# State mixing on 64 rows per head with swapped heads, and TensorE's queue in written order

## The chip, the cores and the metric

The kernel runs on one core of a Trainium2 chip. The metric is device time in microseconds (us) of one execution. Before the change three runs took 2027.13, 2028.16 and 2031.48 us; their median is 2028.16. Engines are called as the profile calls them: PE is TensorE's matmuls and PEld its weight loads, DVE is VectorE, ACT ScalarE, POOL GpSimd, SP the queue from which most transfers are issued.

## What is computed

The reference is a small two-layer transformer trunk over 256 context tokens and 512 latent tokens with 1024 features. The change lies in layer 0, where the mixer has two halves: attention with 8 query heads and 2 key heads, and an RWKV-7 recurrence with 8 heads in two directions over the same tokens. The recurrence keeps a 64x64 state S per head and direction:

```
S_t = S_{t-1} (diag(w_t) - kk_t^T (a_t * kk_t)) + v_t^T k_t ;  y_t = S_t r_t
scan(zero state, context) -> s_ctx ;  scan(s_ctx, latent)      # for d in (forward, reversed)
o = post(y_forward + y_reversed)                               # group norm, bonus, gate
```

Attention for query tiles of the context sees the context alone; for latent tiles it sees all 768 tokens, with a softmax over them.

## The kernel before

The stage in question (lines 882 to 1194) runs state mixing and attention together on TensorE, between the projections of layer 0 and its output projection. It takes the 768 tokens in 24 chunks of 32, two chunks making a block of 64 tokens; both directions go at once, the reversed one from the other end. In memory the 8 heads are 4 tiles of 128 rows, with two heads (h = 0, 1) in the two halves of 64 rows.

`prepare` (L943) loads a block's operands on SP and makes its products. For each direction and each half m of the head tiles, z (L981) multiplies the operands kb by ar. So that one product serves two heads, kb is laid out as a block matrix of 128x128 (the tiles `kbd`, zeroed once, filled by two loads of 64 rows each, L957). Two DVE products (L987) mask z, one into `zk` and one into `z`; ACT copies the rest (L990). xv (L998) multiplies zk by the values v. POOL copies and scales ar into `ard`, laid out as a block matrix too, in four products of 64 rows a block (L972).

`step` (L1007) is the chain from state to state. x (L1022) applies ard to the state, DVE adds xv and gives xs (L1025), u (L1032) applies a triangular inverse in 32x32 tiles, DVE adds v and gives vu (L1037, once per direction), s (L1047) makes the update in 64x64 tiles, and DVE adds it to the decayed old state (L1055), which POOL made (L1013). `outputs` (L1058) makes y from the state and from vu (L1066, L1068) and adds it into `yacc`. `finish` (L1088) normalizes, transposes (yt, L1112), gates and stores a pair of token tiles.

`attend` (L1123) does attention for one query tile: per key head g and query head j the scores sc (L1143, two or four matmuls into one buffer of two PSUM banks), a maximum on DVE (L1145), Exp on ACT (L1150), a scaling; then `weighted` (L323) transposes the probabilities four at a time (pt, L332), copies them out on ACT or DVE alternately (L335, L337), and multiplies them by the values into two halves of po (L341).

What orders the work: the kernel is written as generators. `state_mixing` (L1158) advances attention by 40 yields first and then by a yield here and there between the steps; `step` and the first `prepare` have high priority. The scheduler of the framework then chooses each engine's order by priority and by its own simulated time, so a matmul of any kind can go between two of another. PSUM has two buffers for z, xv, y and yt together, one for x, u and s, one for po, two for pt and one (of two banks) for sc.

Of the kernel before, what the change touches and what calls it, by code (L numbers as in the profile page):

```python
# [38 lines left out]
HALVES = (slice(0, 64), slice(64, 128))  # L39

# [36 lines left out]
def constants():  # L77
# [21 lines left out]
    head, slot = p // 64, (p // 32) % 2  # L99
    own = (head[:, None] == np.arange(2)[None, :])[:, :, None]  # L100
    for dr in (0, 1):
        isk = slot == dr
        sgn = np.where(isk, 1.0, -1.0).astype(f)
        if dr == 0:
            inc, exc = t[None, :] >= s[:, None], t[None, :] > s[:, None]
        else:
            inc, exc = t[None, :] <= s[:, None], t[None, :] < s[:, None]
        c.add(f"rmask{dr}", (own * inc[:, None, :] * sgn[:, None, None]).astype(f))
        c.add(f"kmask{dr}", (own * (exc & isk[:, None])[:, None, :]).astype(f))
        c.add(f"sgn{dr}", sgn)  # L110
        c.add(f"umask{dr}", (~isk).astype(f)[:, None])
# [113 lines left out]
def tile_trunk(ctx: ExitStack, tc: tile.TileContext, t: dict, out, cc: Cols, pc: Cols):  # L225
# [656 lines left out]
    with ExitStack() as sb:  # L882
        psum_pool(sb, zy=(2, 1), ch=(1, 1), po=(1, 1), pt=(2, 1), sc=(1, 2))
# [9 lines left out]
        for g in (0, 1):  # L893
# [3 lines left out]
            split(kh[:, g], kl[:, g], kraw)  # L897
        early = ExitStack()
# [17 lines left out]
        ard = [br.tile([P, 4, 2, 2, 64], F32, name=f"ard{n}") for n in range(5)]  # L916
        zts = [br.tile([P, 4, 2, P], F32, name=f"z{n}") for n in range(4)]
        for n in range(3):
            zero(kbd[n].rearrange("p a c n -> p (a c n)"), n > 1)
            V.tensor_tensor(out=ari[n].rearrange("p a c n -> p (a c) n")[:, :, 64:128], in0=ident[:, 0:64].unsqueeze(1).to_broadcast([P, 8, 64]),  # L920
                            in1=ident[:, 64:128].unsqueeze(1).to_broadcast([P, 8, 64]), op=ALU.add)
        for n in range(5):
            zero(ard[n].rearrange("p a c s n -> p (a c s n)"), n > 1)
# [4 lines left out]
        A.activation(func=AF.Copy, out=dds[:, 0:7, 1, :], in_=DD[1][:, :, 6::-1].rearrange("p a n -> p n a"))  # L928
        A.activation(func=AF.Copy, out=dds[:, 7:23, 1, :], in_=DD[1][:, :, 23:7:-1].rearrange("p a n -> p n a"))
# [13 lines left out]
        def prepare(b):  # L943
# [5 lines left out]
            for d in (0, 1):  # L949
# [3 lines left out]
                kb, ar, bd = kbd[n % 3], ari[n % 3], ard[n % 5]  # L953
                nc.sync.dma_start(ar[:, :, :, 0:64], arD[d][i][:, :, c:c + P].rearrange("q a (c n) -> q a c n", c=2))
                for h in (0, 1):
                    r = HALVES[h]
                    nc.sync.dma_start(kb[r, :, :, 64 * h:64 * h + 64], kbD[d][i, r, :, c:c + P].rearrange("q a (c n) -> q a c n", c=2))  # L957
                    v = vD[64 * blk[d]:64 * blk[d] + 64, h].rearrange("(j q) a e -> q j (a e)", j=2)
                    for j in (0, 1):
                        s = 32 * (2 * h + d)  # L960
                        nc.sync.dma_start(vm[d][s:s + 32, j].rearrange("q a e -> q (a e)"), v[:, 1 - j if d else j, :])
                ld.append((kb, ar))
# [3 lines left out]
            def run():  # L966
                zks = {}
                for d in (0, 1):
                    kb, ar = ld[d]
                    for h in (0, 1):  # L970
                        r = HALVES[h]
                        G.tensor_tensor(out=ars[d][r, :, :, :, 32 * h:32 * h + 32].rearrange("p a c s t -> p (a c) s t"),  # L972
                                        in0=ar[r, :, :, 0:64].rearrange("p a c (s t) -> p (a c) s t", s=2),
                                        in1=dsel[r, b, d].rearrange("p a c -> p (a c)").unsqueeze(2).unsqueeze(3).to_broadcast([64, 8, 2, 32]),
                                        op=ALU.mult)
                    for m in (0, 1):

                        ps = psum("zy", "z")
                        for a in (0, 1):
                            for c in (0, 1):  # L980
                                T.matmul(ps[:, P * (2 * a + c):P * (2 * a + c) + P], lhsT=kb[:, 2 * m + a, c, :], rhs=ar[:, 2 * m + a, c, :],  # L981
                                         start=True, stop=True)
                        pv = ps.rearrange("p (n x) -> p n x", x=P)
                        z = zs[d][:, 2 * m:2 * m + 2].rearrange("p a c x -> p (a c) x")
                        zk = bq.tile([P, 4, 64], F32, tag="zk", name=u("zk"), bufs=4)
                        for dst, c0, nm in ((zk, 32, "kmask"), (z[:, :, 0:64], 0, "rmask")):
                            V.tensor_tensor(out=dst.rearrange("p n (h t) -> p n h t", h=2),  # L987
                                            in0=pv[:, :, c0:c0 + 32].unsqueeze(2).to_broadcast([P, 4, 2, 32]),
                                            in1=K(f"{nm}{d}").rearrange("p (h t) -> p h t", h=2).unsqueeze(1).to_broadcast([P, 4, 2, 32]), op=ALU.mult)
                        A.activation(out=z[:, :, 64:128], in_=pv[:, :, 64:128], func=AF.Copy, scale=K(f"sgn{d}"))  # L990
                        zks[d, m] = zk
                        yield
                for j in (0, 1):
                    px = psum("zy", "xv")
                    for a in range(4):
                        for d in (0, 1):
                            c = 1 - j if d else j
                            T.matmul(px[64 * d:64 * d + 64, 64 * a:64 * a + 64], lhsT=zks[d, a // 2][:, 2 * (a % 2) + c, :], rhs=vm[d][:, j, a, :],  # L998
# [159 lines left out]
        def state_mixing(fill):  # L1158
# [26 lines left out]
            for _ in done:  # L1185
                pass
# [613 lines left out]
```

## Time and profile before

| what | us |
|---|---|
| profiled execution | 2029.69 |
| span of its instructions | 2027.9 |
| median of three runs | 2028.16 |
| PE busy (94% of the span) | 1900.6 |
| DVE busy | 1217.1 |
| ACT busy | 842.6 |
| POOL busy | 360.6 |

The mean granted TensorE clock was 0.975 of full speed. Times inside the span are counted from its first instruction. A float32 matmul appears as two instructions in the trace. An instruction's duration runs from its start to its last result, and matmuls overlap one another in the array, so what a matmul costs is read from one start to the next, not from its duration. A form such as 128*64 128x64 gives the rows and columns of the array that the matmul uses, and then the partitions and the elements that move through it.

### The profile page before, as it was taken

The numbers are of one execution on the slowest core, as the hardware profiler recorded it, in microseconds if no ns is written. First come the engines' busy times: TensorE is split into PE (matmuls) and PEld (weight loads), VectorE is DVE, ScalarE is ACT, GpSimd is POOL, SyncE is SP. The second block draws the span as 40 slices with busy tenths as digits, with TensorE's granted clock in tenths as the row PEclk, the third lists the DMA queues.
The fourth block names the chain that finished last, engine by engine and source line by source line (L and its number), as shares of the span: only waits on it lengthen the run. The fifth ranks groups of instructions, "written<-read, shape, count | busy, mean of one in ns | idle before, by whom it ended". The sixth has DMA issues, their size and how long they took to land.

```text
span 2027.9 us, 34250 instructions
## 1 busy us (share of the span) xinstructions
PE 1900.6 (94%) x13992; PEld 1547.3 (76%) x13992; DVE 1217.1 (60%) x2070; ACT 842.6 (42%) x1419; POOL 360.6 (18%) x371
## 2 busy tenths in 40 slices
PE   6999868899999899999999999899899799999997
PEld 4776647776765898888888889778668487888886
DVE  5577969575677675555544443865677464344436
ACT  4344432455554443332233224554566444333335
POOL 0022276333222430000000002310153120000002
PEclk9999979899999999999999999999899799999998
DMA  9346554842323643344444432212101133323333
GB/s 333 120 146 193 195 174 143 166 98 59 90 59 110 230 124 93 115 125 135 125 126 131 128 94 73 87 45 73 42 1 43 42 95 97 100 86 102 94 99 109
DMA packets 147885, 228.19 MB, mean 113 GB/s; under 512 B 65024, under 2 KB 102288, under 8 KB 147600
## 3 DMA queue, kind: packets, MB, share of 16 engines
q1 hardware_dynamic: 140912, 213.54, 35.8%
q10 hardware_dynamic: 5456, 7.73, 1.1%
q0 software_dynamic: 1360, 4.73, 0.7%
q8 instruction: 110, 1.80, 0.4%
q14 instruction: 47, 0.39, 0.1%
HBM read 200.00 MB, written 25.96 MB: 111 GB/s over the span
## 4 chain that ended last, share of the span: by engine, by line
PE 69%; DVE 13%; DMA 7%; ACT 4%; issue 4%; POOL 3%; SPq 0%; DVEq 0%; POOLq 0%; ACTq 0%
PE m L367 37%; PE win L367 9%; PE po L341 4%; DMA wmod<-in_wmod_dram 4%; PE pt L332 3%; PE z L981 2%; DVE wlo L280 2%; PE wout L1714 2%; PE wout L1298 2%; PE sc L1143 2%; DMA wraw<-in_win_dram 1%; PE z L1556 1%; DVE junk L1315 1%; PE s L1047 1%; DVE it L778 1%
## 5 line engine op out<-in xcount | busy, mean ns | idle before, releaser
L279 ACT ACTIVATE whi<-wraw 128x1024 fp32r<-128x1024 f32 x214 | 226.4, 1059 | 691.1 <-PE m L367 555.7
L280 DVE TENSOR_TENSOR wlo<-wraw,whi 128x1024 fp32r<-128x1024 f32 x214 | 263.7, 1234 | 204.3 <-ACT whi L279 201.5
L367 PE MATMUL m<-hh,whi 128*128 128x512 f32 (+1 forms) x816 | 239.6, 345 | 3.9 <-ACT relu L1237 2.4
L367 PE MATMUL m<-hh,wlo 128*128 128x512 f32 (+1 forms) x816 | 242.1, 345 | 0.4 <-DVE wlo L280 0.4
L367 PE MATMUL m<-hl,whi 128*128 128x512 f32 (+1 forms) x816 | 241.9, 344 | 0.2 <-POOL hl L503 0.2
L367 PE MATMUL m<-dh,whi 128*128 128x256 f32 (+1 forms) x832 | 238.9, 342 | 2.7 <-DVE xl L1219 2.5
L367 PE MATMUL m<-dl,whi 128*128 128x256 f32 (+1 forms) x832 | 241.1, 341 | 0.0
L367 PE MATMUL m<-dh,wlo 128*128 128x256 f32 (+1 forms) x832 | 240.0, 342 | 0.1
L471 POOL TENSOR_TENSOR acc<-acc,nsq 128x256 f32<-128x256 f32 x42 | 43.6, 1047 | 870.9 <-ACT nsq L470 867.0
L367 PEld LDWEIGHTS m<-dh,whi 128*128 128x128 f32 x832 | 153.4, 188 | 24.9 <-DVE xl L1219 6.2
L367 PEld LDWEIGHTS m<-hh,whi 128*128 128x128 f32 x816 | 152.4, 189 | 23.6 <-ACT relu L1237 2.8
L367 PEld LDWEIGHTS m<-hh,wlo 128*128 128x128 f32 x816 | 153.7, 189 | 20.0 <-DVE wlo L280 0.9
L367 PEld LDWEIGHTS m<-hl,whi 128*128 128x128 f32 x816 | 153.8, 189 | 19.2 <-POOL hl L503 0.4
L367 PEld LDWEIGHTS m<-dl,whi 128*128 128x128 f32 x832 | 154.0, 188 | 18.9
L367 PEld LDWEIGHTS m<-dh,wlo 128*128 128x128 f32 x832 | 153.8, 188 | 18.8 <-DVE wlo L280 0.3
L367 PE MATMUL win<-hl,whi 128*128 128x512 f32 (+1 forms) x512 | 162.2, 350 | 4.7 <-POOL hl L503 3.5
L367 PE MATMUL win<-hh,whi 128*128 128x512 f32 (+1 forms) x512 | 158.0, 355 | 8.6 <-DVE kr L381 5.6
L367 PE MATMUL win<-hh,wlo 128*128 128x512 f32 (+1 forms) x512 | 160.3, 347 | 1.8 <-DVE wlo L280 1.8
L1315 DVE SCALAR_TENSOR_TENSOR junk<-wmod,crow 128x1024 f32<-128x1024 f32 x64 | 78.4, 1225 | 119.0 <-DMA wmod<-in_wmod_dram 118.4
L1219 DVE SCALAR_TENSOR_TENSOR xl<-m,modT,xl 128x512 f32<-128x512 f32 (+1 forms) x144 | 97.3, 686 | 72.2 <-PE m L367 72.2
L367 PEld LDWEIGHTS win<-hh,whi 128*128 128x128 f32 x512 | 95.4, 194 | 31.2 <-issue 12.3
L367 PEld LDWEIGHTS win<-hl,whi 128*128 128x128 f32 x512 | 98.9, 194 | 21.1 <-POOL hl L503 4.7
(416 smaller groups left out, 3624.3 us busy)
## 6 DMA issues: line engine op xcount, KB each, us to landing
wraw<-in_w_dram SPq DMA_DIRECT2D x136, 512.0 KB, 3.6
wmod<-in_wmod_dram SPq DMA_DIRECT2D x96, 512.0 KB, 4.1
wraw<-in_wout_dram SPq DMA_DIRECT2D x40, 512.0 KB, 3.7
wraw<-in_win_dram SPq DMA_DIRECT2D x35, 512.0 KB, 4.0
arD<-ar SPq DMA_DIRECT2D x8, 768.0 KB, 4.2
kbD<-kb SPq DMA_DIRECT2D x8, 768.0 KB, 3.7
ari<-arD SPq DMA_DIRECT2D x24, 256.0 KB, 4.3
kbd<-kbD SPq DMA_DIRECT2D x48, 128.0 KB, 4.0
```

The source lines that it names most:

```text
L279: A.activation(out=hi, in_=src, func=AF.Copy)
L280: (lo_eng or V).tensor_tensor(out=lo, in0=src, in1=hi.bitcast(F32), op=ALU.subtract)
L332: T.transpose(pt[:, P * j:P * j + P], prob[j][:, P * m:P * m + P], ident)
L341: T.matmul(po[HALVES[i], :], lhsT=vt[:, k_, r], rhs=w_, start=m_ < 2, stop=m_ + 2 >= n, tile_position=(0, 64 * i))
L367: T.matmul(part(ps, s), lhsT=a[:, c], rhs=row(b, k, s), start=first and j == 0 and q == 0, stop=last and j == n - 1 and q == 2)
L471: (V if k == KT - 1 else eng).tensor_tensor(out=at(acc, s), in0=at(acc, s), in1=at(sq, s), op=ALU.add)
L981: T.matmul(ps[:, P * (2 * a + c):P * (2 * a + c) + P], lhsT=kb[:, 2 * m + a, c, :], rhs=ar[:, 2 * m + a, c, :], start=True, stop=True)
L1143: T.matmul(ps[:, cols2(s)], lhsT=qs[:, 2 * j + g, :], rhs=kx[:, g, s[0]:s[0] + s[1]], start=m == 0, stop=m == 1)
L1219: V.scalar_tensor_tensor(out=xs, in0=part(ps, s), scalar=mod(l, which, m, s[2]), in1=xs, op0=ALU.mult, op1=ALU.add)
L1298: T.matmul(part(ps, s), lhsT=a[:, c], rhs=like(b, s), start=k == 0 and q == 0, stop=k == KT - 1 and q == 2)
L1315: V.scalar_tensor_tensor(out=junk, in0=wm, scalar=1.0, in1=crow[:, :, v], op0=ALU.mult, op1=ALU.mult, accum_out=modT[:, l, n, v:v + 1])
L1714: T.matmul(o, lhsT=a[:, c], rhs=b, start=k == 0 and q == 0, stop=k == KT - 1 and q == 2)
```

## The change

Masks: `rmask` and `kmask`, which had a column block for each head, become one `zmask` of 64 columns. The heads of direction 1 are swapped: head h of direction d sits in rows `HALVES[h ^ d]` of z, ard, the values and the state. A new order lists (head, direction) so that the four land on different parts of the array:

```diff
+HD = ((0, 0), (1, 0), (1, 1), (0, 1))
```

The block matrices go. kb and ard hold 64 rows per head with no zeros; ard is loaded with its rows already swapped and scaled in place:

```diff
-        kbd = [bq.tile([P, 4, 2, P], F32, name=f"kbd{n}") for n in range(3)]
+        kbs = [bq.tile([P, 4, 2, 64], F32, name=f"kb{n}") for n in range(3)]
-        ard = [br.tile([P, 4, 2, 2, 64], F32, name=f"ard{n}") for n in range(5)]
+        ard = [br.tile([P, 4, 2, 2, 32], F32, name=f"ard{n}") for n in range(6)]
...
+                for h in (0, 1):
+                    nc.sync.dma_start(bd[HALVES[h ^ d]].rearrange("q a c s t -> q a (c s t)"), arD[d][i, HALVES[h], :, c:c + P])
```

z is made for both directions together in 64x64 tiles, with one masked copy; zk is now a part of z:

```diff
+                    pz = [psum("z", "z") for _ in (0, 1)]
+                    for a in (0, 1):
+                        for c in (0, 1):
+                            for h, d in HD:
+                                kb, ar = ld[d]
+                                w = P * (2 * a + c)
+                                T.matmul(pz[d][HALVES[h ^ d], w:w + P], lhsT=kb[HALVES[h], 2 * m + a, c, :], rhs=ar[HALVES[h], 2 * m + a, c, :],
+                                         start=True, stop=True, tile_position=(64 * h, 64 * (h ^ d)))
...
+                        V.tensor_tensor(out=z[:, :, 0:64], in0=pv[:, :, 0:64], in1=K(f"zmask{d}").unsqueeze(1).to_broadcast([P, 4, 64]), op=ALU.mult)
```

xv, x and both parts of y run over HD in the same way in tiles of 64 rows and 32 columns at `tile_position=(64 * (h ^ d), 32 * q)` with q = 2d + h; u and s keep their tiles and run over HD:

```diff
-                    for d in (0, 1):
-                        T.matmul(px[64 * d:64 * d + 64, 64 * a:64 * a + 64], lhsT=ars[d][:, a, cl[d], 1, :], rhs=state[:, d, a, :],
-                                 start=True, stop=True, tile_position=(0, 64 * d))
+                    for h, d in HD:
+                        q = 2 * d + h
+                        T.matmul(px[32 * q:32 * q + 32, 64 * a:64 * a + 64], lhsT=ars[d][HALVES[h ^ d], a, cl[d], 1, :], rhs=state[HALVES[h ^ d], d, a, :],
+                                 start=True, stop=True, tile_position=(64 * (h ^ d), 32 * q))
```

Every matmul and transpose of the stage is pinned behind the one written before it on TensorE, and PSUM is divided anew (pt now has one buffer, y one of its own):

```diff
-        psum_pool(sb, zy=(2, 1), ch=(1, 1), po=(1, 1), pt=(2, 1), sc=(1, 2))
+        psum_pool(sb, z=(2, 1), y=(1, 1), ch=(1, 1), po=(1, 1), pt=(1, 1), sc=(1, 2))
...
+            def matmul(self, *args, **kw):
+                tc.keep_in_program_order(nc.tensor.matmul(*args, **kw))
```

The written order of a step n is: x; y of step n-1; u; a slot of attention; z of one half of the next block; s; a second slot. At the end of a block both xv follow, ahead of the next x. Attention is cut into units: the scores of one head, four transposes, or one pair of po matmuls; the values of one key head are merged with the scores of the next. Its probabilities have 9 buffers (5 before), the copies of pt 4 (3), of which DVE makes every third. There are 48 slots and 132 units; a slot advances to a goal that grows evenly:

```diff
+        NU = 12 * 4 + 4 * 3 + 8 * 9
...
+                goal = NU * max(0, i - 2) // 46
+                while taken[0] < goal:
+                    taken[0] += 1
+                    advance(fill)
...
+                    parts = step(state, n, cur, j)
                     with tc.high_priority():
+                        next(parts)
+                    if last:
+                        outputs(*last)
...
+                    with tc.high_priority():
+                        vu = next(parts)
+                    beside(2 * n)
+                    advance(done)
+                    advance(todo)
+                    with tc.high_priority():
+                        new = next(parts)
+                    last = (state, cur, j, vu)
                     state = new
+                    beside(2 * n + 1)
                     advance(done)
+                for _ in todo:
+                    pass
```

The first 40 yields of attention ahead of the steps are gone.

More of the change, by code (lines that the diff above doesn't have):

```diff
@@ L98, in constants @@
     t = np.arange(32)
[L99 to L100 removed]
+    slot = (p // 32) % 2
     for dr in (0, 1):
@@ L1016, in step @@
             xv, vm = xvs[j]
-            hd = [(a, d, h) for a in range(4) for d in (0, 1) for h in (0, 1)]
             if state is not None:
@@ new lines, in values, with pair @@
+        def values(qi, keys, prob, g, o):
+            r, n = HALVES[g], keys[1] - keys[0]
+            po, w = psum("po", "po"), []
+            def pair(m):
+                for i in (0, 1):
+                    T.matmul(po[HALVES[i], :], lhsT=vtok[:, keys[0] + m + i, r], rhs=w[m + i], start=m == 0, stop=m + 2 >= n, tile_position=(0, 64 * i))
+            for m in range(n):
+                pt = psum("pt", "pt")
+                for j in range(4):
+                    T.transpose(pt[:, P * j:P * j + P], prob[j][:, P * m:P * m + P], ident)
+                w.append(tp.tile([P, 512], F32, tag="pts", name=u("pts"), bufs=4))
+                if m % 3 == 2:
+                    V.tensor_copy(out=w[m], in_=pt)
+                else:
+                    A.activation(out=w[m], in_=pt, func=AF.Copy)
+                yield
+                if m % 2 == 0 and m:
+                    pair(m - 2)
+                    yield
+            pair(n - 2)
+            A.activation(out=o[r], in_=po[HALVES[1], :], func=AF.Copy)
+            V.tensor_tensor(out=o[r], in0=po[HALVES[0], :], in1=o[r], op=ALU.add)
+            if g:
+                nc.scalar.dma_start(oD[0:4, :, P * qi:P * qi + P].rearrange("a q c -> q a c"), o.rearrange("p (a c) -> p a c", c=P))
+            yield
@@ new lines, in merge, with attention @@
+        def merge(a, na, b, nb):
+            i = j = 0
+            while i < na or j < nb:
+                if j >= nb or (i < na and i * nb <= j * na):
+                    i += 1
+                    advance(a)
+                else:
+                    j += 1
+                    advance(b)
+                yield
+        def attention():
+            before, nv = iter(()), 0
+            for qi in (0, 1, 3, 4, 2, 5):
+                keys, qs = (0, 2) if qi < 2 else (0, NTT), []
+                o = tp.tile([P, 512], F32, tag="oa", name=u("oa"), bufs=2)
+                for g in (0, 1):
+                    prob = []
+                    yield from merge(before, nv, scores(qi, keys, prob, g, qs), 4)
+                    before, nv = values(qi, keys, prob, g, o), keys[1] * 3 // 2
+            for _ in before:
+                yield
```

192 lines of the change are left out of this document (90 added, 102 removed).

## Prediction

> **What bounds the kernel now.** First the page: busy shares, then the chain that ended last.
>
> ```profile
> span 2027.9 us, 34250 instructions
> PE 1900.6 (94%) x13992; PEld 1547.3 (76%) x13992; DVE 1217.1 (60%) x2070; ACT 842.6 (42%) x1419; POOL 360.6 (18%) x371
> PE 69%; DVE 13%; DMA 7%; ACT 4%; issue 4%; POOL 3%; SPq 0%; DVEq 0%; POOLq 0%; ACTq 0%
> ```
>
> TensorE is the bound overall, but the change touches one stage, so I asked for that stage alone: from the first state product z at 361.1 us to the last y at 641.6, by the windows view.
>
> ```profile
> core 0: us, PE busy (x) PEld busy (x) DVE busy (x) ACT busy (x) POOL busy (x), PEclk, DMA share, GB/s
> 361.00:381.00 20.00, 14.49 (x167) 12.92 (x168) 10.99 (x24) 7.99 (x16) 8.84 (x6) 0.77 1.05 179
> 381.00:641.60 260.60, 255.50 (x3721) 182.43 (x3722) 177.65 (x417) 143.46 (x277) 70.35 (x65) 1.00 0.34 75
> 361.11 2.03 PE L981 MATMUL z<-ari,kbd 128*128 128x128 f32 x16
> 641.28 0.33 PE L1068 MATMUL y<-vu,z 128*64 128x64 f32 x3
> ```
>
> After its first 20 us the stage leaves TensorE idle for only 260.6 - 255.5 = 5.1 us, while VectorE is at 68% and ScalarE at 55%. So fewer array cycles shorten it, if the order lets them. Busy is not the same as streaming, however; a stretch of TensorE's timeline shows what each piece costs (start, us, then the piece; I read start to next start).
>
> ```profile
> 500.90 0.33 PE L332 MATMUL pt<-cst,prob 128*128 128x128 f32 x1
> 501.16 0.34 PE L998 MATMUL xv<-vm,zk 128*64 128x64 f32 x4
> ...
> 505.43 0.50 PE L1032 MATMUL u<-xs,tt 32*32 32x64 f32 x18
> ...
> 506.05 0.39 PE L1143 MATMUL sc<-kh,qs 128*128 128x256 f32 x1
> ...
> 506.94 0.33 PE L1068 MATMUL y<-vu,z 128*64 128x64 f32 x2
> 507.19 1.16 PE L981 MATMUL z<-ari,kbd 128*128 128x128 f32 x8
> 508.28 1.15 PE L1047 MATMUL s<-vu,z 64*64 64x64 f32 x32
> 509.36 0.44 PE L332 MATMUL pt<-cst,prob 128*128 128x128 f32 x2
> 509.73 0.27 PE L1068 MATMUL y<-vu,z 128*64 128x64 f32 x1
> ...
> 511.59 0.69 PE L1022 MATMUL x<-state,ard 128*64 128x64 f32 x16
> 512.20 1.16 PE L981 MATMUL z<-ari,kbd 128*128 128x128 f32 x8
> 513.20 0.38 PE L332 MATMUL pt<-cst,prob 128*128 128x128 f32 x2
> ...
> 515.88 1.08 PE L341 MATMUL po<-pts,vtok 128*64 128x512 f32 x4
> 516.89 0.66 PE L332 MATMUL pt<-cst,prob 128*128 128x128 f32 x4
> 517.48 0.34 PE L1066 MATMUL y<-state,ard 128*64 128x64 f32 x4
> 517.75 1.16 PE L981 MATMUL z<-ari,kbd 128*128 128x128 f32 x8
> ```
>
> Transposes of one shape take 0.26 us alone, 0.37 for two, 0.59 for four: 0.11 each plus 0.15 for the change of shape that follows. With 0.15 taken off every piece that ends in a change: 16 instructions of x take 0.46 (8 pairs of 0.058), the 32 of u (505.43 to 506.05) 0.47 (8 fours of 0.058), the 32 of s 0.93 (16 pairs of 0.058). A z instruction takes 1.00/8 = 0.125 (512.20, no change after), a full score unit 0.74 (506.05 to 506.94), four po instructions 0.86. So small tiles that share no part of the array run side by side, and a group costs the same whether two or four are in it. From 499.8 to 519.1 the full listing has 25 changes of shape: 3.8 us, or some 53 us over 280.
>
> **The change, part by part.** The counts of before, by group:
>
> ```profile
> L981 PE MATMUL z<-ari,kbd 128*128 128x128 f32 x384 | 57.9, 296 | 6.4 <-ACT z L990 5.4 <-ACT xv L1001 0.4
> L341 PE MATMUL po<-pts,vtok 128*64 128x512 f32 x103 | 44.5, 608 | 0.0
> L332 PE MATMUL pt<-cst,prob 128*128 128x128 f32 x212 | 40.3, 290 | 0.0
> L1068 PE MATMUL y<-vu,z 128*64 128x64 f32 x384 | 35.4, 230 | 1.6 <-DVE vu L1037 1.6
> L1066 PE MATMUL y<-state,ard 128*64 128x64 f32 x368 | 30.8, 232 | 0.1
> L1047 PE MATMUL s<-vu,z 64*64 64x64 f32 x736 | 26.4, 222 | 0.0
> L998 PE MATMUL xv<-vm,zk 128*64 128x64 f32 x384 | 20.6, 236 | 0.2 <-ACT z L990 0.2
> L1022 PE MATMUL x<-state,ard 128*64 128x64 f32 x368 | 16.4, 230 | 0.1
> L1145 DVE TENSOR_REDUCE st<-sc 128x1 f32<-128x768 f32 (+1 forms) x48 | 37.2, 776 | 25.9 <-PE sc L1143 25.6
> L987 DVE TENSOR_TENSOR zk<-z,cst 128x256 f32<-128x256 f32 x48 | 20.2, 421 | 16.2 <-PE z L981 15.7
> L1150 ACT ACTIVATE prob<-sc,st,sq 128x768 f32<-128x768 f32 (+1 forms) x48 | 40.7, 847 | 29.3 <-DVE st L1147 22.5 <-PE pt L332 6.5
> L337 ACT ACTIVATE pts<-pt 128x512 f32<-128x512 f32 x27 | 16.0, 594 | 30.5 <-PE pt L332 30.5
> ```
>
> *State products, now without zeros.* z used the whole array on a block matrix that is half zeros; now four 64x64 tiles fill the four quarters. Instructions double to 768, but go four abreast: 192 x 0.125 = 24 us for 48. x, y and xv become twice as many instructions on 64x32 tiles, four abreast instead of two: the same number of groups, so 10.7, 21.8 and 11.1 us as before. u stays 11.1 and s 21.3 (its order still gives pairs). Together 100 us.
>
> Four abreast is shown by u on 32x32 tiles only. Two 64-row tiles in one bank run abreast too: the 32 of s, on diagonal quarters of one bank, take 1.08 us. [...]
>
> *Attention.* The units are 48 of scores, 56 of four transposes, 28 of a po pair. Up to the last y, three of the 132 are left out: scores 32 x 0.74 + 16 x 0.37 = 29.6, transposes 220 x 0.11 = 24.2, po 26 x 0.86 = 22.4: 76 us, with 1.8 for yt 78. The po pairs are now always issued together; before, 103 instructions kept TensorE busy for 44.5 us where paired ones need 103/4 x 0.86 = 22, so many ran singly.
>
> *Changes of shape.* In written order a step has five (y to u, u to attention, attention to z and s, s to attention, attention to xv and x); 24 steps give 120, and 28 po pairs inside pieces of 128-wide work some 39 more: 159 x 0.15 = 24 us.
>
> *Waits of an in-order queue.* Nothing can now slip past a waiting matmul, so every unit behind it waits too. Waits come from: the start, where z, its masks, xv and u of block 0 follow one another and block 1's operands must land before s of step 0, with no attention for three slots (before: 5.5 us idle at clock 0.77; I take 14); score units next to each other among the first 25 units, sharing one sc buffer (reduce, scale and Exp of the short form, some 1.4 us, 8 places: 11); a transpose unit or po pair right behind a transpose unit with the single pt buffer (evacuation 0.59 and the way there, 0.9; 16 places, two thirds inside a slot: 10, and 3 at the end); the chain xs, vu, state where a 0.78 us reduction stands ahead on VectorE, 0.5 a step: 11. Together 49 us; none of it is in the trace of before. Bounds: 20 if the slots cover all but start and end, 90 if each of 46 slots loses about 1.5 us besides.
>
> *Beside TensorE, at nothing.* The 48 zk masks (20.2 us of VectorE) go, and some ten copies of transposed probabilities (0.6 us each) move from VectorE to ScalarE; GpSimd's four half-partition products a block become two. VectorE comes to 189 - 20 - 6 = 163 us and ScalarE to 151 + 6 = 157, 65% and 63% of a 250 us stage: off the bound. Two more loads a block and direction lengthen SP's queue, where they stand ahead of the other direction's operands.
>
> ```profile
> ari<-arD SPq DMA_DIRECT2D x24, 256.0 KB, 4.3
> ```
>
> A load lands 4.3 us after its issue; a step (251/24, some 10 us) lies between the release of the buffers and the z that reads them. Should that cover fail, z waits in order, 2 us a block by my estimate (24 in all), which the upper bound of the waits holds.
>
> *Sum.* 100 + 78 + 24 + 49 = 251 us from 361, so the last y at 612 instead of 641.6: 29 us. What follows:
>
> ```profile
> 641.60:680.20 38.60, 30.07 (x201) 24.50 (x198) 27.66 (x41) 17.54 (x23) 10.59 (x9) 0.94 0.74 235
> 670.89 5.73 DMA raw<-oD
> 680.21 7.55 PE wout L1298 x40
> ```
>
> The last third of the output projection waits for the last y through normalization, a store and this load: 38.6 us from y to 680.2, of which TensorE is busy for 30, so it could not start sooner than this chain ends. The change leaves the chain alone, so the 29 us carry over. The profiled execution took 2029.69 us, 1.8 of them outside its span; the median of the three runs is 2028.16, and from that the forecast is 1999 us.
>
> **The rivals.** *The queue flows (15%).* Slots of about 1.7 us and y (0.93) cover every chain, as VectorE and ScalarE at two thirds would allow; waits of 20 us instead of 49: 1970. Against it: one sc and one pt buffer.
>
> *The queue stands (15%).* A score unit finds its buffer held by Exp, which waits for the reduction on VectorE, both behind other work in their own in-order queues: reduce 0.78, Exp 0.85, scale and hops 0.5 make 2.1 us, and another 1.8 with one operation ahead on each. Between two score units lie on average 5 us, so this bites only where the engines lag. It decides from 78 us of waits on (1.7 per slot), where the gain is gone; at its price of 90 us: 2040, slower. For it: ScalarE's probability chain already waits 29.3 us in before.
>
> *Two abreast (7%).* 64-row tiles that share columns or rows with a neighbour do not run in fours but in pairs, which doubles the groups: z +24, x +10.7, y +21.8, xv +11.1, together 68 us: 2067. For it: no row of before has four such tiles. Against it: u in fours, and x, whose two tiles share all rows. [...]
>
> **How the numbers follow.** My forecast has 63%: 1999, by itself 1981 to 2017 (waits 31 to 67). A measurement here tells 0.2% (4 us) from nothing. Forecast and first rival are faster: 78%. Of the rest 4% lie within 0.2% and 18% above. The range runs from 1974 (most of the smooth case) to 2036 (the standing queue without its end); two abreast is left out.
>
> **What would show it.** Right: z rows of 16 or 32 instructions in 64x64 tiles at about 0.03 us each; x followed by y with no gap; shape changes halved; last y near 612; idle time of TensorE in the stage near 50 us, ended by ScalarE (pts, prob) and VectorE. Wrong: z at 0.06 per instruction (two abreast), idle beyond 78 us, or a stage that is shorter while the output projection still begins where it did.

## The result, and the profile after

| | median, us | runs | lowest to highest |
|---|---|---|---|
| before | 2029.82 | 4 | 2027.13 to 2032.96 |
| after | 2312.6 | 4 | 2311.85 to 2322.39 |

The changed kernel is slower: the ratio is 1.140, with a 95% interval of 1.137 to 1.144. The forecast was 1999 us. The profiled execution after is the longest of the four, 2322.39 us, with a mean clock of 0.907 (before 0.975).

The page of the changed kernel, first its span and TensorE, then the shares of the chain that ended last:

```profile
span 2320.6 us, 37865 instructions
PE 1946.3 (84%) x15880; PEld 1585.8 (68%) x15880; DVE 1207.1 (52%) x2010; ACT 846.9 (36%) x1429; POOL 319.4 (14%) x343
PE 60%; DVE 8%; ACT 8%; issue 4%; POOL 2%; DMA 1%; SPq 0%; POOLq 0%; DVEq 0%; ACTq 0%
```

Busy time grew by 46 us, but the span by 293: TensorE stands idle for 374 us instead of 127, and its share of the last chain fell from 69 to 60%. To see where, I cut both runs at the same events (last y, first matmul m of layer 0's MLP, first tok transpose of layer 1, first cb, last po, end) and asked for each stretch. The first number after the stretch is its length, then come the busy times of PE, PEld, DVE, ACT and POOL, the granted clock, the DMA share and GB/s. Before:

```profile
641.60:735.30 93.70, 83.17 (x620) 76.60 (x618) 69.82 (x107) 47.38 (x73) 43.00 (x38) 0.95 0.70 225
735.30:1320.20 584.90, 573.33 (x3484) 510.46 (x3483) 308.70 (x472) 182.68 (x240) 31.28 (x32) 0.99 0.37 110
1320.20:1475.90 155.70, 147.92 (x819) 114.09 (x817) 97.03 (x178) 77.87 (x133) 17.43 (x24) 0.97 0.17 51
1475.90:1627.00 151.10, 133.62 (x783) 98.63 (x782) 98.59 (x191) 90.37 (x218) 50.75 (x56) 0.92 0.09 29
1627.00:2027.90 400.90, 382.81 (x1921) 323.32 (x1920) 192.28 (x256) 161.06 (x241) 22.85 (x22) 0.99 0.33 99
```

After, with the stage itself ahead of them:

```profile
363.80:671.20 307.40, 234.16 (x5783) 174.31 (x5784) 171.72 (x382) 157.30 (x306) 54.74 (x48) 0.87 0.40 98
671.10:783.80 112.70, 85.15 (x619) 81.12 (x616) 76.50 (x118) 49.54 (x77) 43.21 (x38) 0.86 0.56 185
783.80:1400.20 616.40, 582.86 (x3478) 514.37 (x3478) 300.70 (x455) 175.97 (x230) 26.80 (x30) 0.97 0.30 101
1400.20:1673.70 273.50, 188.24 (x845) 140.44 (x846) 112.83 (x202) 92.23 (x159) 21.51 (x34) 0.77 0.10 32
1673.70:1887.90 214.20, 153.56 (x756) 116.25 (x754) 88.12 (x169) 82.20 (x196) 36.55 (x46) 0.79 0.06 20
1887.90:2320.60 432.70, 391.95 (x1921) 330.20 (x1920) 195.05 (x256) 161.85 (x241) 21.16 (x22) 0.96 0.28 92
```

The last y lies at 671.1 us instead of 641.6, so about 30 us are lost up to the end of the stage. Behind it, where the diff touches nothing, every stretch is longer: by 19.0, 31.5, 117.8, 63.1 and 31.8 us, 263 together. There the number of instructions is the same within a few per cent. Idle time grew by 182 us, and busy time by 81 at a lower clock (0.77 instead of 0.97 in the stretch with the largest loss). The waits of TensorE between 1400 and 1674 us say which kind (total, times, longest):

```profile
PE tok L906 <- DVE xf L1473: 36.0, 4, 9.0
PE pt L906 <- ACT prob L1613: 9.5, 2, 7.6
PE sc L903 <- ACT prob L1601: 9.0, 11, 1.6
```

The line numbers give the cause away. L903 and L906 are the two lines of `InOrder`, the helper that pins a matmul to the written order, and matmuls of layer 1 stand on them. The diff binds `T = InOrder()` inside the stage, but `T` is the variable through which every later matmul of the kernel is issued, and nothing sets it back. Transposes to token order wait for VectorE (36.0 us for xf) with nothing allowed past them; in the kernel before, the scheduler had put other projections ahead, and the same view has no wait of these transposes for xf.

In the stage the waits are these (the largest rows, and the gaps that end for no reason that the profile shows):

```profile
PE sc L903 <- ACT prob L1162: 11.5, 8, 2.5
PE pt L906 <- ACT pts L1185: 11.3, 10, 2.2
PE pt L906 <- ACT prob L1164: 9.1, 5, 3.3
PE y L903 <- issue: 8.6, 4, 2.7
PE u L903 <- DVE xs L1032: 6.7, 6, 2.9
PE z L903 <- DMA kb<-kbD: 4.8, 1, 4.8
PE x L903 <- ACT state L1062: 4.6, 1, 4.6
```

With the smaller rows such waits come to 73 us; before, the stage had 9. The products behave as forecast: where TensorE runs at full clock, 32 instructions of z pass in 0.93 us and 32 of x in 0.47, with y right behind, and the changes of shape fell from 331 to 151.

```profile
609.05 1.10 PE L903 MATMUL z<-ari,kb 64*64 64x128 f32 x32
609.98 1.10 PE L903 MATMUL s<-vu,z 64*64 64x64 f32 x32
...
612.95 0.65 PE L903 MATMUL x<-state,ard 64*32 64x64 f32 x32
613.42 0.63 PE L903 MATMUL y<-state,ard 64*32 64x64 f32 x32
...
615.04 0.66 PE L906 MATMUL pt<-cst,prob 128*128 128x128 f32 x4
```

### The profile page after: what moved, and what is told of

It reads as the page before. It is cut to its first block, busy times and chain, and to the rows that moved or that the text cites. A ratio compares the mean times of both kernels' runs of the same rounds, so it can differ in the third digit from the quotient of the medians.

```text
span 2320.6 us, 37865 instructions
## 1 busy us (share of the span) xinstructions
PE 1946.3 (84%) x15880; PEld 1585.8 (68%) x15880; DVE 1207.1 (52%) x2010; ACT 846.9 (36%) x1429; POOL 319.4 (14%) x343
## 3 DMA queue, kind: packets, MB, share of 16 engines
q8 instruction: 125, 2.05, 0.4%
## 4 chain that ended last, share of the span: by engine, by line
PE 60%; DVE 8%; ACT 8%; issue 4%; POOL 2%; DMA 1%; SPq 0%; POOLq 0%; DVEq 0%; ACTq 0%
PE m L903 36%; PE win L903 5%; PE wout L903 4%; PE po L903 3%; PE sc L903 2%; PE pt L906 2%; PE z L903 2%; DVE wlo L281 1%; ACT whi L280 1%; DVE conv L1469 1%; ACT prob L1162 1%; PE yd L903 1%; DVE st L1157 1%; PE y L903 1%; PE s L903 1%
## 5 line engine op out<-in xcount | busy, mean ns | idle before, releaser
L903 PE MATMUL m<-dh,whi 128*128 128x256 f32 (+1 forms) x832 | 246.6, 346 | 8.1 <-ACT dh L280 7.3
L903 PE MATMUL m<-dl,whi 128*128 128x256 f32 (+1 forms) x832 | 245.0, 344 | 5.0 <-DVE dl L281 5.0
L903 PE MATMUL m<-hh,whi 128*128 128x512 f32 (+1 forms) x816 | 245.4, 347 | 2.2 <-ACT relu L1323 2.2
L903 PE MATMUL m<-dh,wlo 128*128 128x256 f32 (+1 forms) x832 | 244.9, 344 | 0.6 <-DVE wlo L281 0.6
L903 PE MATMUL m<-hh,wlo 128*128 128x512 f32 (+1 forms) x816 | 245.4, 347 | 0.0
L903 PE MATMUL m<-hl,whi 128*128 128x512 f32 (+1 forms) x816 | 243.8, 345 | 0.0
L903 PEld LDWEIGHTS m<-dh,whi 128*128 128x128 f32 x832 | 155.7, 190 | 31.9 <-ACT dh L280 13.7
L903 PEld LDWEIGHTS m<-dl,whi 128*128 128x128 f32 x832 | 155.5, 190 | 28.7 <-DVE dl L281 9.9
L903 PEld LDWEIGHTS m<-hh,whi 128*128 128x128 f32 x816 | 155.6, 191 | 22.7 <-ACT relu L1323 2.6
L903 PEld LDWEIGHTS m<-dh,wlo 128*128 128x128 f32 x832 | 156.0, 190 | 20.2 <-DVE wlo L281 0.8
L903 PEld LDWEIGHTS m<-hl,whi 128*128 128x128 f32 x816 | 155.5, 191 | 19.6
L903 PEld LDWEIGHTS m<-hh,wlo 128*128 128x128 f32 x816 | 155.2, 190 | 19.5 <-DVE wlo L281 0.3
L906 PE MATMUL pt<-cst,prob 128*128 128x128 f32 x368 | 72.9, 323 | 47.8 <-ACT prob L1613 16.7
L368 PE MATMUL win<-hh,whi 128*128 128x256 f32 (+1 forms) x336 | 104.3, 353 | 7.0 <-DVE kr L382 5.1
L368 PE MATMUL win<-hl,whi 128*128 128x256 f32 (+1 forms) x336 | 107.6, 349 | 0.0
L368 PE MATMUL win<-hh,wlo 128*128 128x256 f32 (+1 forms) x336 | 106.6, 348 | 0.6 <-DVE wlo L281 0.6
L906 PEld LDWEIGHTS pt<-cst,prob 128*128 128x128 f32 x368 | 48.7, 162 | 80.7 <-ACT prob L1613 19.4
```

The lines of the kernel that those rows point to most:

```text
L368: T.matmul(part(ps, s), lhsT=a[:, c], rhs=row(b, k, s), start=first and j == 0 and q == 0, stop=last and j == n - 1 and q == 2)
L903: tc.keep_in_program_order(nc.tensor.matmul(*args, **kw))
L906: tc.keep_in_program_order(nc.tensor.transpose(*args, **kw))
```

## The experiments

Each ratio is to the kernel before, run on the same chip.

| kernel | median, us | ratio, 95% interval | last y, us |
|---|---|---|---|
| pin ends with the stage | 2051.32 | 1.0099 (1.0078 to 1.0120) | 665.1 |
| no pin at all | 2020.33 | 0.9952 (0.9939 to 0.9965) | 637.3 |
| kernel before, pinned behind the stage | 2292.5 | 1.1285 (1.1260 to 1.1311) | 647.0 |
| pin ends, two pt buffers | 2034.78 | 1.0023 (1.0010 to 1.0036) | 649.6 |
| no pin, 16 pieces ahead | 2010.55 | 0.9918 (0.9905 to 0.9930) | 628.9 |
| pin ends, two pt buffers, three slots | 2048.66 | 1.0103 (1.0087 to 1.0118) | 666.1 |
| no pin, 16 ahead, two pt buffers | 2023.52 | 0.9975 (0.9966 to 0.9985) | 641.0 |
| 16 ahead, state products pinned | 2047.44 | 1.0096 (1.0078 to 1.0114) | 665.0 |
| 16 ahead, attention pinned | 2022.2 | 0.9964 (0.9950 to 0.9979) | 646.0 |
| no pin, 40 ahead | 2006.87 | 0.9898 (0.9883 to 0.9913) | 624.4 |
| state products pinned, none ahead | 2044.72 | 1.0076 (1.0047 to 1.0105) | 662.0 |
| pin ends, idle filled at the start | 2047.15 | 1.0087 (1.0059 to 1.0114) | 668.0 |
| pin ends, half of y three times | 2089.32 | 1.0302 (1.0286 to 1.0317) | 702.1 |
| pin ends, y split | 2049.43 | 1.0101 (1.0084 to 1.0118) | 669.9 |
| no pin, 40 ahead, half of y three times | 2071.82 | 1.0215 (1.0197 to 1.0233) | 684.7 |

### Where the pin holds

**The pin ends with the stage.** One line behind the call:

```diff
         state_mixing(attention())
+        T = nc.tensor
```

> The changed kernel, but the written order of TensorE ends with the state mixing: behind it the matmuls are handed out by the scheduler again. Theory A (the pin stays in force for the rest of the program, and that is where about 253 of the 283 us lie): the stage stays as in the changed kernel (last y near 671 us), everything behind it takes as long as in the kernel before, so about 2030 + 29 = 2059 us. Rival B (what was lost behind the stage comes from something else, the lower clock or the layout of memory that the stage leaves): it stays above 2250 us. Rival C (half and half): 2100 to 2200 us, and the stretches behind the stage tell which stayed long.

**The pin behind the stage alone**, put into the kernel before, at the end of its stage:

```diff
+    class InOrder:
+        def matmul(self, *args, **kw):
+            tc.keep_in_program_order(nc.tensor.matmul(*args, **kw))
...
+    T = InOrder()
```

> The kernel before, with its stage as it was and TensorE in written order only from the end of the state mixing on. Theory A: the pin behind the stage alone costs about 253 us, so about 2283 us, with last y at 642 us as before. Rival B (the loss behind the stage needs the new stage ahead of it): about 2030 us. In between, 2100 to 2200 us, the new stage and the pin would share it.

Two stretches of the kernel whose pin ends, then the one of layer 1 in the kernel before with the pin behind:

```profile
757.30:1337.50 580.20, 571.41 (x3484) 509.53 (x3483) 309.06 (x471) 182.71 (x239) 30.51 (x32) 0.99 0.34 111
1337.50:1494.60 157.10, 149.19 (x819) 114.57 (x817) 96.79 (x178) 77.91 (x133) 17.46 (x24) 0.96 0.15 51
```

```profile
1376.30:1644.90 268.60, 183.36 (x849) 137.10 (x849) 112.41 (x202) 92.43 (x160) 21.62 (x34) 0.79 0.11 32
```

With the pin ended, 580.2 and 157.1 us stand where before has 584.9 and 155.7: the loss behind the stage is gone to the last stretch. With the old stage and the pin behind it, layer 1's stretch takes 268.6 us, near the changed kernel's 273.5, and the whole loses 262 us, 258 of them behind the last y. Theory A holds from both sides: 258 of the 263 us come without the new stage. Two smaller differences were not forecast. With the pin ended the last y comes at 665.1 us and not at 671, although the program of the stage is the same; gaps that end for no reason that the profile shows come to 10.7 us instead of 15.7 and make most of the difference. With the pin behind the old stage the last y comes 5 us later than before, and I do not know why.

### What the stage is worth without the pin

**No pin at all:**

```diff
-        T = InOrder()
```

> The changed kernel without any written order: the new layout on 64 rows per head, TensorE's instructions handed out by the scheduler throughout. Theory A (the layout is worth its shorter products, and the in-order waits of the stage, 73 us, are what turned it into a loss): last y between 600 and 640 us and the whole kernel at 1985 to 2030 us. Rival B (the layout needs the written order: without it fours of small products mix with attention pieces and each change of shape costs): last y above 660 us, the whole above 2050 us.

What is left of the change without the pin gains 0.5% (the layout with its masks, and also attention in units with its buffers, and the new division of PSUM; no run has the layout by itself), and the written order of the stage costs 31 us (2051.3 against 2020.3). In this run's stage TensorE is idle for 28 us instead of 69, at a clock of 0.98 instead of 0.89, though it changes shape 300 times instead of 152:

```profile
364.00:637.40 273.40, 245.47 (x5769) 170.30 (x5769) 166.58 (x382) 154.84 (x304) 53.92 (x48) 0.98 0.46 107
364.00:665.20 301.20, 232.21 (x5788) 172.76 (x5789) 172.22 (x383) 157.27 (x306) 54.15 (x48) 0.89 0.41 100
```

(The first line is without the pin, the second with the pin ended.) Nearly half of the 28 us without the pin lie in the first 25 us. The timeline there shows ACT waiting 4.42 us for a late load of the queries, and TensorE behind it for the copy of z:

```profile
384.87 1.06 ACT L1146 ACTIVATE qs<-qr 128x1024 fp32r<-128x1024 f32 x1 [4.42 <-DMA qr<-qD]
385.83 0.82 ACT L997 ACTIVATE z<-z,cst 128x256 f32<-128x256 f32 x2
...
386.34 1.06 PE L991 MATMUL z<-ari,kb 64*64 64x128 f32 x10 [6.58 <-ACT z L997]
```

**16 and 40 pieces of attention ahead of the steps**, as the kernel before had 40:

```diff
-        state_mixing(attention())
+        fill = attention()
+        for _ in range(16):
+            advance(fill)
+        state_mixing(fill)
```

> The new layout without any written order, with the first 16 pieces of attention handed out ahead of the state mixing, as the kernel before does with its first 40. In the run without the pin TensorE stood 11 us of the first 21 us of the stage: ACT waited there 4.42 us for the load of the queries (qs after qr), and with it the copies of z that TensorE waits for (6.58 us at 379.8). Theory A (the start waits for loads that are issued late, not for the layout): the idle time between 364 and 385 us falls to 3 to 6 us, last y comes 5 to 9 us sooner than 637, and the whole takes 2010 to 2015 us. Rival B (the start is bound by the chain z, xv, u, s itself): unchanged within 2 us of 2020.

> As the free order with 16 pieces of attention ahead, with 40 as in the kernel before. Theory A (the start needs only that the queries are loaded and some scores stand ready; 16 do that): within 3 us of 2010.6. Rival B (more pieces ahead fill more of the waits of the first 60 us): 2003 to 2007 us. Rival C (attention that is ahead leaves nothing to fill the end of the stage): 2014 us or more.

Both are faster, 2010.6 and 2006.9 us, by 0.8 and 1.0% with intervals below 1. With 16 ahead the time and the last y came out as theory A had them, but not for its reason: between 364 and 385 us the idle time fell from 11.3 to 9.9 us and not to 3 to 6, and most of the gain lies behind 385 us. With 40 ahead the waits in the stage come to 13 us, and the stage takes 262 us with 303 changes of shape:

```profile
362.00:624.50 262.50, 248.69 (x5771) 172.63 (x5772) 166.21 (x382) 154.15 (x304) 54.41 (x48) 0.95 0.45 112
```

That is the best kernel of the study, 1.0% faster than the kernel before: what the change is worth without its order. Whether 40 pieces are better than 16 the intervals leave open; they overlap a little.

**Two buffers for pt in free order.** 

> As the free order with 16 pieces ahead, and two PSUM buffers for the transposed probabilities, y sharing z's two. Theory A (in free order the scheduler already finds other work where the one buffer is taken, so the second adds nothing): within 3 us of the kernel with the 16 pieces. Rival B (the second buffer is worth in free order what it was worth in written order, 16 us): about 1998 us. Rival C (y and z now wait for each other): 5 us or more slower.

13 us slower than with one, and the last y comes 12 us later: rival C by its size. Its reason is not seen, since y waits only some 1.5 us for the copies of z and xv, which share its buffers now. Idle time rose from 24 to 30 us, most of it at scores that wait for Exp (6.2 us instead of 1.1) and at x, which waits for the state (4.1 instead of 1.0), and busy time from 242 to 247. Why is not shown.

### What in the written order costs

**Two buffers for pt in written order**, y sharing z's:

```diff
-        psum_pool(sb, z=(2, 1), y=(1, 1), ch=(1, 1), po=(1, 1), pt=(1, 1), sc=(1, 2))
+        psum_pool(sb, z=(2, 1), ch=(1, 1), po=(1, 1), pt=(2, 1), sc=(1, 2))
...
-            py = psum("y", "y")
+            py = psum("z", "y")
```

> As the kernel whose pin ends with the stage, and in the stage the transposed probabilities get two PSUM buffers; y takes one of z's two instead of its own. Theory A (11 us of waits on the copies of the transposed probabilities, and some clock lost behind each of them, go): last y 12 to 20 us sooner than in the kernel with the pin ended, near 655 us, and the whole at about 2043 us. Rival B (what waits there is late next for the probabilities themselves, or y now waits for z's copies): last y within 4 us of 671, the whole unchanged at about 2059 us.

The waits for the copies of pt (11.6 us) are gone, and 16.5 us of the total: theory A. The same edit, 16 us better here and 13 worse in free order, shows that a buffer's worth hangs on the order around it.

**Three slots a step** in that kernel, one of them between y and u:

```diff
+                    beside(3 * n)
                     with tc.high_priority():
                         vu = next(parts)
-                    beside(2 * n)
+                    beside(3 * n + 1)
...
-                    beside(2 * n + 1)
+                    beside(3 * n + 2)
```

> As the kernel with the pin ended and two buffers for the transposed probabilities (2035 us, last y 650), but the attention is put at three places of each step instead of two: between y and u as well, so that at most 64 to 96 small instructions stand in a row, and about two pieces at a place instead of three. Theory A (the idle time that waits for nothing the profile shows, 13 us in that kernel, comes from instructions that are fetched too slowly where 128 small ones stand in a row; the waits for the probabilities come from pieces that stand side by side): these gaps fall under 5 us, the waits for probabilities from 24 to under 15 us, against some 25 more changes of shape at about 0.12 us (3 us): 2015 to 2025 us. Rival B (the gaps have another cause, and the waits only move): gaps and waits stay over 30 us together, 2035 to 2045 us.

Slower by 14 us. The unexplained gaps fell from 11.7 to 6.8 us, not quite under 5, but the waits for probabilities rose from 24 to 33: of the two parts of theory A the second was wrong. The time lies above both ranges; the idle time, 67 us, is rival B's.

**Which half of the pin?** Pinned among themselves are the state products alone, in free order with 16 pieces ahead and with none, and attention's products alone, with 16 ahead. The edit for the first; z, xv, x, u and y go the same way:

```diff
-        T = InOrder()
+        S = InOrder()
...
-                    T.matmul(pd[r, 256 * d + 64 * a:256 * d + 64 * a + 64], lhsT=zs[d][r, a, cl[d], 64:128], rhs=vu[d][r, a, :],
+                    S.matmul(pd[r, 256 * d + 64 * a:256 * d + 64 * a + 64], lhsT=zs[d][r, a, cl[d], 64:128], rhs=vu[d][r, a, :],
```

> As the free order with 16 pieces of attention ahead (2010.6 us, last y 629), but the state products z, xv, x, u, s and y are pinned among themselves; the attention is free to go between them. Theory A (what the written order costs in the stage is that attention pieces, too, stand in the row and wait for their copies and probabilities with nothing allowed past them): with the attention free, idle time stays under 35 us, the clock of the stage above 0.95, last y at 630 to 640 us, the whole within 10 us of 2011. Rival B (the order of the state products themselves is what costs: x, y and xv wait for one another): idle time above 45 us and the whole above 2030 us.

> As the free order with 16 pieces ahead, but the attention's own products (sc, pt, po) are pinned among themselves and the state products are free. Theory A (the waits for probabilities and for the copies of pt stop the attention alone, and the state products fill the gaps while there are any): idle time 25 to 40 us, the whole 2012 to 2025 us. Rival B (attention in written order is the whole cost of the pin in the stage): last y near 650 to 665 us and the whole 2035 to 2050 us.

> The new layout without pieces of attention ahead, with the state products pinned among themselves and the attention free (in the run with 16 pieces ahead the first z stood behind those pieces, at 408.8 us instead of 364, so that run does not tell what the order of the state products costs). Against 2020.3 us with nothing pinned and 2051.3 with both pinned. Theory A (the attention in the row is what costs): 2020 to 2030 us, idle time of the stage under 40 us. Rival B (the state products' own order costs): 2040 us or more, with idle time over 50 us that ends at state products (z, u, x, y). Rival C (half of each, since a pinned product also cannot go ahead of attention that stands before it in the program): 2030 to 2040 us.

I had attention down as the culprit, and that fell. Attention pinned costs 11.6 us (2022.2 against 2010.6). The first run with state products pinned can't be read, since they stayed behind the 16 pieces that stand ahead of them in the program:

```profile
380.61 0.55 PE L1155 MATMUL sc<-kh,qs 128*128 128x256 f32 x1 [16.85 <-DVE qs L1148]
...
408.83 1.44 PE L903 MATMUL z<-ari,kb 64*64 64x128 f32 x32
```

Without pieces ahead it can: 2044.7 us against 2020.3 with nothing pinned and 2051.3 with all, so 24 of the 31 us come with the state products' order. Its idle time is 54 us, but only some 20 of it end at state products by a named releaser, as rival B had it; 11.6 are unexplained gaps, and 22.5 end at attention's products, which were free in this run; that no state product might go ahead of them there is my reading.

**Does idle time lower the clock?** Needless products of 128x128 fill the first step's gaps:

```diff
+            def warm(n):
+                pw = psum("y", "warm")
+                for k in range(n):
+                    T.matmul(pw[:, 0:P], lhsT=ident, rhs=ident, start=True, stop=True)
```

> As the kernel whose pin ends with the stage (2051.3 us; clock 0.67 from 364 to 385 us), with idle times of the first step filled by needless products of 128 by 128: 8 between the first two z, 24 ahead of xv, 28 behind the first u and 28 behind the first s; their results are read by nobody. Theory A (TensorE's clock falls because it stands idle): the granted clock of 364 to 385 us rises to 0.9 or more, and the products behind them take what they take at full clock: the second z's 32 in 0.9 to 1.0 us instead of 1.46, xv's 64 in 1.1 instead of 1.93, the first x's 32 in 0.65 instead of 1.08 and y's 32 in 0.65 instead of 1.11; last y 0 to 5 us sooner than 665. Rival B (the clock falls with the kind of products, four small ones abreast): clock under 0.75 and the same products as long as before, last y later by what the fillers add, 0 to 6 us.

Pin ended, without filling (the window's columns as above):

```profile
366.81 1.46 PE L903 MATMUL z<-ari,kb 64*64 64x128 f32 x32 [1.16 <-ACT z L998]
372.29 1.93 PE L903 MATMUL xv<-vm,z 64*32 64x64 f32 x64 [4.02 <-ACT z L998]
388.56 1.08 PE L903 MATMUL x<-state,ard 64*32 64x64 f32 x32 [4.59 <-ACT state L1062]
364.00:385.00 21.00, 9.86 (x230) 8.34 (x229) 8.08 (x16) 4.97 (x9) 2.63 (x1) 0.67 0.91 201
```

And with it:

```profile
366.94 1.10 PE L903 MATMUL z<-ari,kb 64*64 64x128 f32 x32
373.52 1.10 PE L903 MATMUL xv<-vm,z 64*32 64x64 f32 x64
391.33 0.65 PE L903 MATMUL x<-state,ard 64*32 64x64 f32 x32
364.00:385.00 21.00, 20.02 (x321) 18.65 (x318) 5.52 (x10) 4.96 (x9) 1.83 (x1) 0.96 0.83 178
```

The same instructions take 1.93 us or 1.10, 1.08 or 0.65, by whether TensorE stood idle ahead of them (4.02 and 4.59 us); the granted clock from 364 to 385 us is 0.67 without the filling and 0.96 with it. In the changed kernel, whose program of the stage is the one without the filling, xv's 64 take 1.93 us as well, at a granted clock of 0.50 (372.2 to 374.0 us). On the clock theory A holds, and the kind of products is out as its cause. The whole did not change beyond the intervals (1.0087 against 1.0099), and the last y came 3 us later where theory A had it sooner; the fillers stand in the queue too.

**The unexplained gaps.** They lie in the middle of small products, here among y's 32 in the changed kernel:

```profile
599.91 0.61 PE L903 MATMUL y<-vu,z 64*32 64x64 f32 x26
603.17 0.31 PE L903 MATMUL y<-vu,z 64*32 64x64 f32 x6 [2.65 <-issue]
```

The transfers in this gap (600.5 to 603.2 us) and then in the whole run, by queue, have a row for the one that carries instructions (transfers, MB, share):

```profile
q8 instruction: 1, 0.02, 2.8%
q8 instruction: 125, 2.05, 0.4%
```

One transfer of 2.05 MB / 125 = 16 KB. In three kernels I changed the number of small products in a row: y's first half made three times in written and in free order (two of the three for nothing), and y's second half moved behind the first slot.

```diff
-            if state is not None:
+            for k in range(3 if state is not None else 0):
...
-                                 start=a == 0, stop=False, tile_position=(64 * (h ^ d), 32 * q))
+                                 start=a == 0, stop=k < 2 and a == 3, tile_position=(64 * (h ^ d), 32 * q))
```

```diff
-                    if last:
-                        outputs(*last)
+                    rest = outputs(*last) if last else iter(())
+                    next(rest, None)
...
                     beside(2 * n)
+                    next(rest, None)
```

> As the kernel whose pin ends with the stage (2051.3 us, last y 665.1; 10.7 us of idle time in gaps over 0.3 us that end for no reason the profile shows), but y's first half is made three times over, the first two times for nothing: 64 more small products in a row per step, so up to 192 instead of 128. At full clock 32 of them take 0.45 us, 46 such groups 21 us. Theory A (the unexplained gaps come from small instructions that TensorE uses up faster than they are fetched): these gaps grow to 30 us or more, and last y comes 35 to 60 us later. Rival B (the gaps have another cause, such as a transfer or a semaphore that the trace does not show): they stay at 7 to 15 us, and last y comes 18 to 25 us later.

> As the kernel whose pin ends with the stage (2051.3 us), but y's second half stands behind the first slot of attention, so that at most 96 small products stand in a row instead of 128. Theory A (fetching): the unexplained gaps, 10.7 us there, fall under 5 us, and last y comes 0 to 6 us sooner than 665, with some 3 us lost to one more change of shape a step. Rival B (another cause): 8 to 14 us of gaps as before.

> As the free order with 40 pieces of attention ahead (2006.9 us, last y 624.4; 2.2 us of unexplained gaps), with y's first half made three times over as well. Theory A (fetching too slow where small products stand together; the scheduler spreads them less well when there are more): gaps of 8 to 25 us, last y 25 to 45 us later. Rival B (no limit in the fetching): gaps under 5 us, last y 18 to 25 us later for the products themselves.

The gaps grew from 10.7 to 25.3 us with up to 192 in a row, fell to 5.4 with at most 96, and in free order rose from 2.1 to 13.3. Their largest row with y made three times, against 5.5 us in 3 gaps before it:

```profile
PE y L903 <- issue: 16.4, 10, 3.3
```

So they grow when more small instructions stand close together; rival B's constant gaps are out, though 25.3 is less than theory A's 30 (its last y, 37 us later, lies in theory A's range). The fall to 5.4 says less: it lies in neither range, and the same program of the stage gave 15.7 us of gaps in the changed kernel and 10.7 with the pin ended.

Where the gaps stand in the traces says what they wait for. The instruction queue moved 125 transfers of 16 KB for 31,960 instructions of TensorE (matmuls, weight loads and its semaphore instructions), and 136 for 34,926 with y made three times: one for every 256. If TensorE's instructions are numbered by their start, 8 of the 9 unexplained gaps in the changed kernel's stage come at one and the same place of every 256, at a multiple of 256 plus 193 or 194; so do 15 of the 16 with y made three times and 9 of the 10 in free order with y three times, and each of these ends 1.2 to 1.7 us after such a transfer has ended. By place and time the gaps go with the fetching of instructions: theory A. Why most blocks of 256 cost nothing and some up to 3.4 us is not shown.

In the free kernel the last y came 60 us later, more than either theory gave it; 29 of them are idle time and 28 busy time, of which the added products are some 21. The split itself gained nothing (the last y came 5 us later), since y's second half no longer covers DVE's xs: u waits 16.4 us for it instead of 6.8.

## Why the prediction was wrong

**The step that failed: "the 29 us carry over".** The whole sum was made for the stage, and all behind it was taken to be as before. My description had the pin as one on "every matmul and transpose of the stage"; the diff shows where it is bound, and not where it is released, and I did not follow the variable past the last line of the hunk. The stretches above put 263 of the 293 us there, and two runs show it from both sides: with the pin ended the loss behind the stage is gone, and with the pin behind the old stage 258 us are lost there. No rival of mine lay behind the stage either.

**The stage: 251 us forecast, 307 measured.** It also began 2.7 us later. Even with the pin ended it was a loss where a gain of 29 us was forecast. Three terms were off: 24 us of waits, some 6 of prices, and a clock that the sum had at nothing, some 26.

*Waits: 49 forecast, 73 measured.* The four places I named were there at about their size: the start 14.8 us for 14, adjacent score units 11.5 for 11, the single pt buffer 13.9 for 13 (11.3 at transposes, 2.6 at po), xs 6.7 for the chain's 11. What I did not name made the difference: transposes whose probabilities were not ready, 9.1 us, and gaps in rows of small instructions, 15.7. The loads of block 1 that z waits for (4.8 us) are in the start; I counted two more loads a block and direction, where the diff has one more, since the two of kb became one. The rival of the standing queue was to break even at 78 us of waits; at 73 the stage was already 30 us late, since the other terms were too low.

*Products, attention and changes: 202 forecast.* If the time from start to next start, idle taken off, is added up over all of TensorE's rows of the stage by kind, the changed kernel has 126 us for state products and 108 for attention and yt, changes of shape included: 234. The same sum for the kernel before gives 161 and 109, that is 270, where my prices (124 + 78 + 332 x 0.15) give 252. So the list was some 18 us too low for the kernel that I had in hand, and I never held it against that. From the one kernel to the other it gives 50 us less and the rows 36, at a lower clock. For the changed kernel most of the difference is the clock: instructions that start at a granted clock of 1.00 hold 177 of the 234 us, and if those that start at 0.50 are put at the mean of their kind at 1.00, the sum is 208, 6 more than forecast (an estimate from the rows). Pairing po gained less than I saw in it: 105 instructions took 35 us, 32 at that mean, against 38 before and 22 forecast; the rows contain the changes of shape around them, the forecast does not.

*The clock: not priced at all.* I took durations from rows at clock 1.00 and then forecast 49 us of idle time beside them. The stage ran at a mean of 0.87. By the same estimate the 57 us of instructions that start at 0.50 would take some 31 at 1.00, so the clock cost about 26 us; the run with the filled gaps shows it row by row (xv's 64 in 1.93 us behind idle time, in 1.10 without).

**What held.** Fours of 64-row tiles do run abreast: 32 instructions of z in 0.93 us (two banks, two row tiles in each) and 32 of x in 0.47 (one bank, two row tiles in it). Two abreast is out. VectorE and ScalarE stayed off the bound (172 and 157 us of 307; 163 and 157 were forecast). Without the pin the rest of the change does make the kernel faster: 2006.9 us with 40 pieces of attention ahead, where I had forecast 1999 for the change as a whole.

**What stays open.** Why some blocks of instructions cost a gap and most do not; how the 24 us of the state products' order divide between those gaps, the clock and products that may not pass one another; and what the layout is worth by itself.

## What to carry to other kernels

Before you price a change, follow each name that it binds to the end of the program: here one variable that was not set back cost nine times what the stage did. Hold a list of prices against the kernel in hand before you use it on the next one, and price idle time twice, once for itself and once for the slower clock behind it (in this stage 73 us of waits and, by the estimate above, about 26 us of clock). The order fixed by hand saved 150 changes of shape and 13 us of busy time, and cost 41 us of idle time (2051.3 us against 2020.3 without it).

## What the hardware showed that I had not expected

The clock answered to idle gaps of a few microseconds: with the pin ended, 64 products of xv took 1.93 us behind a gap of 4.02 us, and 1.10 with the gap filled; the granted clock from 364 to 385 us was 0.67 and 0.96. In the changed kernel the 64 took 1.93 us behind a gap of 4.17 us, at a granted clock of 0.50. A shorter gap stood ahead of a slow stretch, too: there the clock was 0.50 from 396.34 to 399.75 us, behind a gap of 1.70 us that ended at 396.12.

TensorE used up small instructions faster than they arrived: in the changed kernel the 128 products of x, y and u, with as many weight loads, pass in some 2.1 us where nothing holds them (612.95 to 615.04), and 8 of the stage's 9 unexplained gaps, of up to 2.7 us, stand at one and the same place of every 256 instructions. The forecast had no term for these gaps; they came to 15.7 us there, to 10.7 with the pin ended, and to 25.3 with more small products.
